# Stick-breaking logits from stacked float32r parts, and a new place for a GpSimd product, in a two-block mixer kernel

## Chip, cores and metric

The kernel runs on 1 core of one Trainium2 chip. Its metric is the device time of one execution in microseconds; "before" is the median of three runs, 1353.47 us (1352.7 to 1354.14).

## What is computed

Two blocks follow each other on a sequence of 256 tokens with 1024 channels. The first block has two layers. Each projects the normalised input `u` with one wide matrix and runs three mixers on it, A (top-k attention), B (windowed attention with sinks) and C (stick-breaking attention), gates them, merges them and adds the result to the input. The change lies in mixer C and its inputs:

```python
z = jnp.einsum('bthd,bshd->bhts', qb, k).astype(jnp.float32) * (dh ** -0.5)
log_beta = jax.nn.log_sigmoid(z)
log_1m = jnp.where(strict, jax.nn.log_sigmoid(-z), 0.0)
after = lax.cumsum(log_1m, axis=3, reverse=True) - log_1m
a = jnp.where(strict, jnp.exp(log_beta + after), 0.0)
```

There are 8 heads of 64 channels. The second block has two layers of four mixers on this stream and a context stream; its shift, scale and gate columns (`mod`) come from a matrix `w_ada_2` times a conditioning vector.

## The kernel before, in words

**Tiles.** Activations lie with channels on the partitions. A projection works on one weight tile of 256 columns: `wtile` (L226) loads it in two raw halves (`raw`, L215, on the SP queue, three buffers `wr`), ScalarE rounds each half to float32r (`wh`), VectorE takes the remainder (`wl`), four buffers each. `proj_ch` (L276) and `proj_tok` (L265) then run 48 matmuls of 256 columns, three for each product: high x high, low x high, high x low. Their PSUM pool has three buffers. Everything whose line is L107 is a matmul, whatever called it.

**Mixer C.** In `block1` (L619 to 628) two tiles give `cqT` (scaled by 1/8) and two give `ckT`, each [128, 4, 256] in float32: head 2c + a lies in chunk c on the partitions 64a to 64a + 63. Two tiles of values `cv` and two of the gate (`cg`) follow, then `stick` (L744). For each pair of chunks q and each half a it runs one pass of logits: for both key blocks s and both chunks j one float32 matmul over the 64 rows of the half, of 256 columns for s = 0 and 128 for s = 1, and after each s a bf16 mask matmul of the 256 columns on the diagonal (L759 to 762). There are 4 passes in a layer and 8 in the kernel. Between passes ScalarE, VectorE and TensorE work out logarithms, sums over later keys and exponentials.

**Mixer B** holds its parts already in float32r: `queries` (L448) cuts a tile of rotated queries into a high and a low part in the shared buffer `stg` (one buffer) and sends both with four DMAs of the SP queue to opposite halves of the two tiles `bq`; the keys, twice on the partitions, are `bk[0]` (high) and `bk[1]` (low). A logit is then two matmuls over 128 rows (`logit`, L469). `bq` lies in the places a7 and s1, `bk` in b1 and s2. A place (a tag of the pool `keep`) holds one tile at a time; a new tile in it waits until the old one was read for the last time, in the order of the program.

**GpSimd's jobs.** `ada` (L289) prepares the columns `mod` of a later layer. A job `wide` (L317) covers 512 columns: four loads `wsp` of 256 rows on the SP queue (two places, t3a and t3b), for each half k and each of nv conditioning vectors a product with a column of the vector and an addition to `acc`. With nv = 2 (the second block's) the first vector's product goes to `wc`, a tile in `stg`, and the second's overwrites `wsp` (L332 to 334). After the job `end` (L336) sums the columns of `acc` over the partitions on TensorE and VectorE writes `mod` (L342).

**What sets the order.** The tile framework puts waits between instructions in program order, and a planner fixes the order on each engine's queue at build time by an estimated timeline (`schedule_with_timeline_sim=True`, L1487). `after_tile` (L238) is called after each projection tile of `block1`. In layer 1 a counter starts at 1.0 and grows by 0.11 a call, and whenever it reaches 1 a job is taken from the list: at calls 1, 10, 19 and 28. Calls 1 to 18 are the tiles of aq/ak, av, ag, cq, ck, cv, cg, bq and bkv; mixer B stands between calls 18 and 19, calls 19 and 20 are the tiles of bg, 21 and later the merge. `end` of a job follows 10 calls later, ordered behind the last matmul at that point. In layer 0 the jobs have nv = 1 and don't use `wc`. At the end of `block1` the halves of `cT` (L1386) are loaded into t3a and t3b; the second block's context stream (`hch`, `hcl`, L525 and 526) needs `cT` and the first 16 columns of `mod`.

Of the kernel before, what the change touches and what calls it, by code (L numbers as in the profile page):

```python
# [8 lines left out]
F32 = mybir.dt.float32  # L9
F32R = mybir.dt.float32r  # L10
BF = mybir.dt.bfloat16
U8 = mybir.dt.uint8
AF = mybir.ActivationFunctionType
OP = mybir.AluOpType
# [10 lines left out]
            cq=3652, ck=4164, cv=4676, cg=5188, ma=5700, mb=6724, mc=7748)  # L25
# [33 lines left out]
class Net:  # L59
# [229 lines left out]
    def ada(self, l, blk):  # L289

        nc = self.nc
        nv = 1 if blk == 1 else 2
        wa = self.I["w_ada" if blk == 1 else "w_ada_2"][l]
        v0 = blk - 1
        mod = self.const.tile([128, 24, nv], F32, name=f"mod{blk}{l}")

        def load(n):
            return [self.raw(wa, k, n * 256, 256, True) for k in (0, 4)]

        def job(n, ws=None):  # L300
            ws = ws or load(n)
            bias = self.colB[:, 48 * (blk - 1) + 24 * l:48 * (blk - 1) + 24 * l + 24]
            p = self.P(self.pj, [128, 512])
            for k in range(8):
                g = 32 * (k % 4)
                self.mm(p[g:g + 32, :256], self.cs[:, k, :], ws[k // 4][:, k % 4, :], start=k < 4, stop=k >= 4)
            sb = self.W("adas", [128, 256], tag="score")
            nc.scalar.activation(sb, p[:, :256], AF.Copy)
            pc = self.P(self.tr, [128, 2, 4, 32])
            for j in range(2):  # L310
                self.T(pc[:, j].rearrange("p g v -> p (g v)"), sb[:, 128 * j:128 * j + 128])
            r = self.W("adar", [128, 2, nv])
            nc.vector.tensor_reduce(r, pc[:, :, :, v0:v0 + nv].rearrange("p j g v -> p j v g"), axis=AX.X, op=OP.add)
            nc.vector.scalar_tensor_tensor(mod[:, 2 * n:2 * n + 2, :], r, 0.5,
                                           bias[:, 2 * n:2 * n + 2][:, :, None].to_broadcast([128, 2, nv]),
                                           op0=OP.mult, op1=OP.add)
        def wide(n, tag):  # L317

            P = nc.gpsimd
            acc = self.K("acc", [128, 2, 512], tag=tag)  # L320
            for c in range(4):
                w = self.K("wsp", [128, 2, 512], tag=self.spare[self.nspare % len(self.spare)])
                self.nspare += 1
                nc.sync.dma_start(out=w, in_=wa[256 * c:256 * c + 256, 512 * n:512 * n + 512].rearrange(
                    "(k p) n -> p k n", p=128))
                for k in range(2):
                    for v in range(nv):
                        m = self.cs[:, 2 * c + k, v0 + v:v0 + v + 1]
                        if c == k == 0:
                            P.tensor_scalar(acc[:, v], w[:, k], m, None, op0=OP.mult)  # L330
                        else:
                            t = self.W("wc", [128, 512], tag="stg") if v + 1 < nv else w[:, k]  # L332
                            P.tensor_scalar(t, w[:, k], m, None, op0=OP.mult)  # L333
                            P.tensor_tensor(acc[:, v], acc[:, v], t, op=OP.add)  # L334

            def end():  # L336
                p = self.P(self.tr, [128, 4, 32])
                for j in range(4):
                    for v in range(nv):
                        self.mm(p[:, j, v:v + 1], acc[:, v, 128 * j:128 * j + 128], self.ones[:, 0:1])  # L340
                bias = self.colB[:, 48 * (blk - 1) + 24 * l:48 * (blk - 1) + 24 * l + 24]
                nc.vector.scalar_tensor_tensor(mod[:, 4 * n:4 * n + 4, :], p[:, :, :nv], 0.5,  # L342
                                               bias[:, 4 * n:4 * n + 4][:, :, None].to_broadcast([128, 4, nv]),
                                               op0=OP.mult, op1=OP.add)
            self.later.append((6 if nv == 1 else 10, end))

        return (mod, [lambda ws=None, n=n: job(n, ws) for n in range(12)], [lambda n=n: wide(n, ("s4", "w1")[n % 2]) for n in range(6)],
                load)

# [98 lines left out]
    def queries(self, Q, c0, src, scale):  # L448

        g = self.W("stg", [128, 2, 2, 256], F32R)  # L450
        self.tok_to_ch_split(g[:, 0], g[:, 1], src, scale)
        for a in range(2):
            r = slice(64 * a, 64 * a + 64)
            for i in range(2):
                o = 64 * (a ^ i)
                self.nc.sync.dma_start(out=Q[a][o:o + 64, c0:c0 + 2].bitcast(F32), in_=g[r, i].bitcast(F32))

    def quads(self, dst, src, scale, parts):

# [68 lines left out]
    def block1(self, l, xT, mod, pre):  # L528
        nc, V, A = self.nc, self.nc.vector, self.nc.scalar
        wi = self.I["w_in"][l]  # L530
        r = self.rstd_row(xT, EPS)
# [4 lines left out]
        u = self.pair("u", ("uh", "ul"))  # L536
# [13 lines left out]
        w = self.wtile(wi, OFF1["idx"], pre=pre.get("idx"))  # L550
# [12 lines left out]
        w = self.wtile(wi, OFF1["idx"] + 256, 68, pre=pre.get("iw"))  # L563
# [8 lines left out]
        for t in range(2):  # L572
# [3 lines left out]
            for a in range(2):  # L576
                p = self.P(self.lg, [128, 2, 256])
                b = 64 * a
# [37 lines left out]
        gate("a")  # L616
        self.finish1(ysA, gT["a"], Y["a"])

        cqT = self.K("cqT", [128, 4, 256], tag="a4")  # L619
        ckT = self.K("ckT", [128, 4, 256], tag="a5")  # L620
        for nm, dst, sc in (("cq", cqT, 0.125), ("ck", ckT, 1.0)):
            for i, w in tiles(nm, 2):
                A.activation(dst[:, 2 * i:2 * i + 2], self.proj_ch(w, u), AF.Copy, scale=sc)
        cv = self.K("cv", [128, 2, 512], tag="a6")
        for i, w in tiles("cv", 2):
            A.activation(cv[:, :, 256 * i:256 * i + 256], self.proj_tok(w, 256, u), AF.Copy)
        gate("c")
        self.stick(cqT, ckT, cv, gT["c"], Y["c"])

        bq = [self.K("bq", [128, 4, 256], F32R, tag=t) for t in ("a7", "s1")]  # L630
        bk = [self.K("bk", [128, 2, 256], F32R, tag=t) for t in ("b1", "s2")]
        bv = self.K("bv", [128, 2, 128], tag="b2")
        for i, w in tiles("bq", 2):
            ro = self.W("ro", [128, 2, 4, 64])
# [106 lines left out]
            self.nc.scalar.activation(ys[t], y, AF.Copy)  # L741
        return ys

    def stick(self, qT, kT, v, g, Y):  # L744

        nc, V, A = self.nc, self.nc.vector, self.nc.scalar
        sl = [(slice(None), slice(None), slice(128 * s, 256)) for s in range(2)]
        for q in range(2):
            es = self.K("ste", [128, 4, 2, 256], tag="at")
            for a in range(2):  # L750
                b = 64 * a
                ps = []
                x = self.K("stx", [128, 768], tag=("s3", "n2")[a])
                xs = [x[:, :512].rearrange("p (j t) -> p j t", j=2), x[:, 512:].rearrange("p (j t) -> p j t", j=2)]
                for s in range(2):
                    p = self.P(self.lg, [128, 2, 256])
                    for j in range(2):
                        c = 2 * q + j
                        self.mm(p[:, j, 128 * s:], kT[b:b + 64, c, s * 128:s * 128 + 128],  # L759
                                qT[b:b + 64, c, 128 * s:], start=j == 0, stop=False)  # L760
                    self.mm(p[:, :, 128 * s:128 * s + 128], self.identb,
                            self.bandm[:, 0:1].to_broadcast([128, 2, 128]), start=False, stop=True)
                    ps.append(p)
                    ins = A.activation(xs[s], p[sl[s]], AF.Abs)
# [727 lines left out]
```

## Time and profile before

| | |
|---|---|
| median of three runs | 1353.47 us |
| the profiled execution | 1352.58 us |
| its span, first to last instruction | 1350.8 us |
| mean granted TensorE clock | 0.972 |
| busy: TensorE matmul, VectorE, ScalarE, GpSimd | 95%, 67%, 48%, 29% |
| DMA | 217.65 MB, mean 161 GB/s |

In the profile PE is TensorE's matmuls, PEld its weight loads, DVE VectorE, ACT ScalarE, POOL GpSimd, SPq the queue that issues the DMAs. A float32 matmul leaves two matmul records, a float32r one leaves one. Matmuls overlap, so their pace is read from start to start. A releaser behind "<-" is what ended the idle time before an instruction.

### The profile page before, as it was taken

How to read it: one execution, taken by the hardware profiler on the slowest of the kernel's cores; microseconds unless marked ns; L12 is line 12 of the kernel's file. 1: busy time of each engine (PE TensorE's matmuls, PEld its weight loads, DVE VectorE, ACT ScalarE, POOL GpSimd, SP SyncE). 2: the span in 40 equal slices, each digit the busy share in tenths (PEclk: the TensorE clock that was granted, in tenths of full speed). 3: DMA queues.
4: the chain of work that ended last, by engine and by line, in shares of the span. 5: the costliest groups of instructions: out<-in, count | busy, mean ns of one | idle time of the engine just before them, and what ended most of it. 6: DMA issues, size and time to landing. Idle time of an engine off the chain costs nothing.

```text
span 1350.8 us, 27852 instructions
## 1 busy us (share of the span) xinstructions
PE 1277.5 (95%) x11386; PEld 1163.7 (86%) x11386; DVE 908.9 (67%) x1717; ACT 648.8 (48%) x1160; POOL 393.9 (29%) x233
## 2 busy tenths in 40 slices
PE   6999999999998999999998999999899999999986
PEld 2988988999898898899997988987789789999775
DVE  3897675665679855486675376754748768696873
ACT  3445456644444545764453233334736646434652
POOL 0484984150098921949500010000000000000000
PEclk8899999999989999999998999999899998999997
DMA  9764885476645575446664554326244255654220
GB/s 327 252 203 141 250 244 166 137 243 211 179 143 170 150 209 161 141 155 209 208 208 142 155 157 133 91 94 172 77 142 140 74 161 156 188 159 109 79 79 32
DMA packets 199599, 217.65 MB, mean 161 GB/s; under 512 B 10800, under 2 KB 183472, under 8 KB 198832
## 3 DMA queue, kind: packets, MB, share of 16 engines
q1 hardware_dynamic: 199472, 215.87, 53.2%
q8 instruction: 90, 1.47, 0.5%
q14 instruction: 37, 0.30, 0.1%
HBM read 199.06 MB, written 4.19 MB: 150 GB/s over the span
## 4 chain that ended last, share of the span: by engine, by line
PE 72%; DVE 12%; issue 6%; SPq 4%; DMA 3%; ACT 3%; POOL 0%; POOLq 0%; ACTq 0%; DVEq 0%
PE ps L107 68%; PE ps L111 4%; DVE wl L115 3%; SPq L466 2%; DMA wr<-w_in 2%; SPq L222 1%; DVE pe L703 1%; DVE nm L482 1%; DVE score L589 1%; ACT pe L487 1%; DMA wsp<-w_ada 1%; ACT wh L114 1%; DVE m L588 1%; DVE ro L428 1%; DVE score L584 0%
## 5 line engine op out<-in xcount | busy, mean ns | idle before, releaser
L115 DVE TENSOR_TENSOR wl<-wr,wh 128x1024 fp32r<-128x1024 f32 (+1 forms) x270 | 357.6, 1326 | 226.9 <-ACT wh L114 223.3
L114 ACT ACTIVATE wh<-wr 128x1024 fp32r<-128x1024 f32 (+1 forms) x270 | 284.9, 1056 | 349.3 <-PE ps L107 200.0
L107 PE MATMUL ps<-uh,wh 128*128 128x256 f32 x704 | 201.8, 287 | 3.4 <-ACT thm L659 3.4
L107 PE MATMUL ps<-ul,wh 128*128 128x256 f32 x704 | 201.2, 286 | 0.0
L107 PE MATMUL ps<-uh,wl 128*128 128x256 f32 x704 | 200.7, 285 | 0.0
L333 POOL TENSOR_SCALAR wsp<-wsp,cs 128x512 f32<-128x512 f32 x70 | 137.3, 1967 | 20.9 <-DMA wsp<-w_ada 20.9
L107 PEld LDWEIGHTS ps<-uh,wh 128*128 128x128 f32 x704 | 132.8, 189 | 5.8 <-ACT thm L659 4.4
L107 PEld LDWEIGHTS ps<-ul,wh 128*128 128x128 f32 x704 | 132.7, 188 | 3.1 <-issue 2.9
L107 PEld LDWEIGHTS ps<-uh,wl 128*128 128x128 f32 x704 | 132.8, 189 | 1.5 <-issue 1.1
L107 PE MATMUL ps<-wh,uh 128*128 128x256 f32 (+1 forms) x416 | 121.3, 293 | 1.8 <-ACT uh L525 1.4
L107 PE MATMUL ps<-wl,uh 128*128 128x256 f32 (+1 forms) x416 | 121.0, 292 | 1.5 <-DVE wl L115 1.5
L107 PE MATMUL ps<-wh,ul 128*128 128x256 f32 (+1 forms) x416 | 120.4, 290 | 0.4 <-DVE ul L526 0.4
L334 POOL TENSOR_TENSOR acc<-acc,wsp 128x512 f32<-128x512 f32 x70 | 107.8, 1540 | 2.5
L487 ACT ACTIVATE pe<-ps,nm 128x512 f32<-128x512 f32 (+2 forms) x160 | 85.0, 542 | 42.3 <-DVE nm L482 29.3
L397 POOL TENSOR_TENSOR rec<-rec,mhalf 128x8 f32<-128x8 f32 (+1 forms) x10 | 15.4, 1544 | 293.9 <-DVE rec L396 193.8
L482 DVE TENSOR_REDUCE nm<-ps 128x1 f32<-128x512 f32 (+2 forms) x104 | 70.8, 685 | 26.3 <-PE ps L107 24.7
L107 PEld LDWEIGHTS ps<-wh,uh 128*128 128x128 f32 x416 | 82.1, 198 | 3.7 <-ACT uh L525 1.6
L107 PEld LDWEIGHTS ps<-wl,uh 128*128 128x128 f32 x416 | 82.2, 198 | 2.8 <-DVE wl L115 1.8
L107 PEld LDWEIGHTS ps<-wh,ul 128*128 128x128 f32 x416 | 82.1, 198 | 0.8 <-DVE ul L526 0.7
L379 POOL TENSOR_TENSOR rc<-rc,mhalf 128x2 f32<-128x2 f32 x6 | 5.0, 833 | 255.4 <-DVE rc L378 255.4
L107 PE MATMUL ps<-wl,hxh 128*128 128x256 f32 x256 | 73.2, 286 | 0.5 <-DVE wl L115 0.5
L107 PE MATMUL ps<-wh,hxh 128*128 128x256 f32 x256 | 73.2, 286 | 0.1
(377 smaller groups left out, 3526.3 us busy)
## 6 DMA issues: line engine op xcount, KB each, us to landing
wr<-w_in SPq DMA_DIRECT2D x204, 512.0 KB, 4.1
wsp<-w_ada SPq DMA_DIRECT2D x68, 512.0 KB, 5.0
wr<-w_out SPq DMA_DIRECT2D x40, 512.0 KB, 3.5
wr<-w_ada SPq DMA_DIRECT2D x28, 512.0 KB, 4.5
wr<-w_br_a SPq DMA_DIRECT2D x8, 512.0 KB, 3.6
wr<-w_br_c SPq DMA_DIRECT2D x8, 512.0 KB, 4.0
wr<-w_br_b SPq DMA_DIRECT2D x8, 512.0 KB, 4.3
kC<-stg SPq DMA_DIRECT2D x64, 64.0 KB, 2.1
```

Of the source, the lines that this page charges most:

```text
L107: self.last_mm = self.nc.tensor.matmul(o, l, r, start=start, stop=stop, skip_group_check=True).ins
L111: self.nc.tensor.transpose(o, i, self.ident[:n, :n])
L114: self.nc.scalar.activation(h, x, AF.Copy)
L115: self.nc.vector.tensor_tensor(l, x, h, op=OP.subtract)
L222: self.nc.sync.dma_start(out=w[:, :, :n], in_=ap[k0 * 128:k0 * 128 + 512, c0:c0 + n].rearrange("(k p) n -> p k n", p=128))
L333: P.tensor_scalar(t, w[:, k], m, None, op0=OP.mult)
L334: P.tensor_tensor(acc[:, v], acc[:, v], t, op=OP.add)
L397: self.nc.gpsimd.tensor_tensor(r, r, self.mhalf[:, :r.shape[1]], op=OP.pow)
L428: V.tensor_tensor(dst, t1, b, op=OP.add)
L466: self.nc.sync.dma_start(out=d[32 * i:32 * i + 32].bitcast(F32), in_=g[32 * j:32 * j + 32, part].bitcast(F32))
L482: nc.vector.tensor_reduce(nmx, p, axis=AX.X, op=OP.max, negate=True)
L487: nc.scalar.activation(e[:, j, :], p[:, j, :], AF.Exp, bias=nm[:, h:h + 1], accum_out=ss[:, h:h + 1])
```

## The change

`cq` becomes two pairs of tiles, one for the high parts and one for the low parts, and `ck` one pair; each pair has a tile for each half a. `heads_ch` rounds the projection to a high part (ScalarE) and takes the low part (VectorE) in `stg`, then sends them with DMAs of SP: each part of the queries to both halves of the partitions (8 DMAs a tile), the keys' high part to the head's own half and the low part to the other half (4 a tile). A logit is two float32r matmuls over 128 rows, the stacked keys with the queries' high parts and with their low parts. The product low x low, left out in the kernel's other products, is part of it. `wc` moves from `stg` to the place w2; `bq[1]` moves from s1 to a3 and `bk[1]` from s2 to w2.

```diff
@@ wide
-                            t = self.W("wc", [128, 512], tag="stg") if v + 1 < nv else w[:, k]
+                            t = self.K("wc", [128, 512], tag="w2") if v + 1 < nv else w[:, k]
@@ new functions
+    def parts_of(self, g, l, p, scale):
+        self.nc.scalar.activation(g, p, AF.Copy, scale=scale)
+        self.nc.vector.scalar_tensor_tensor(l, p, scale, g, op0=OP.mult, op1=OP.subtract)
...
+    def heads_ch(self, dst, c0, p, scale):
+        g = self.W("stg", [128, 2, 2, 256], F32R)
+        self.parts_of(g[:, 0], g[:, 1], p, scale)
+        for a in range(2):
+            r = slice(64 * a, 64 * a + 64)
+            for i, o in ((i, o) for i in range(2) for o in range(2)):
+                if len(dst) == 2 or i == (o != a):
+                    self.nc.sync.dma_start(out=dst[i % len(dst)][a][64 * o:64 * o + 64, c0:c0 + 2].bitcast(F32),
+                                           in_=g[r, i].bitcast(F32))
+
+    def head_products(self, o, qs, k, start, swap=False):
+        for n, q in enumerate(qs):
+            self.mm(o, *((k, q) if swap else (q, k)), start=start and n == 0, stop=False)
@@ block1
-        cqT = self.K("cqT", [128, 4, 256], tag="a4")
-        ckT = self.K("ckT", [128, 4, 256], tag="a5")
-        for nm, dst, sc in (("cq", cqT, 0.125), ("ck", ckT, 1.0)):
+        stack = lambda n, tags: [self.K(n, [128, 4, 256], F32R, tag=t) for t in tags]
+        cq = (stack("cqh", ("a4", "a5")), stack("cql", ("t1", "t2")))
+        ck = (stack("ck", ("s1", "s2")),)
+        for nm, dst, sc in (("cq", cq, 0.125), ("ck", ck, 1.0)):
             for i, w in tiles(nm, 2):
-                A.activation(dst[:, 2 * i:2 * i + 2], self.proj_ch(w, u), AF.Copy, scale=sc)
+                self.heads_ch(dst, 2 * i, self.proj_ch(w, u), sc)
...
-        self.stick(cqT, ckT, cv, gT["c"], Y["c"])
-        bq = [self.K("bq", [128, 4, 256], F32R, tag=t) for t in ("a7", "s1")]
-        bk = [self.K("bk", [128, 2, 256], F32R, tag=t) for t in ("b1", "s2")]
+        self.stick(cq, ck[0], cv, gT["c"], Y["c"])
+        bq = [self.K("bq", [128, 4, 256], F32R, tag=t) for t in ("a7", "a3")]
+        bk = [self.K("bk", [128, 2, 256], F32R, tag=t) for t in ("b1", "w2")]
@@ stick
-                        self.mm(p[:, j, 128 * s:], kT[b:b + 64, c, s * 128:s * 128 + 128],
-                                qT[b:b + 64, c, 128 * s:], start=j == 0, stop=False)
+                        self.head_products(p[:, j, 128 * s:], [x[a][:, c, 128 * s:] for x in Q],
+                                           K[a][:, c, s * 128:s * 128 + 128], j == 0, True)
```

## Rows read from the trace of the kernel before

**Rows 1.** The page: engines' busy time, and the chain that ended last by engine
```profile
PE 1277.5 (95%) x11386; PEld 1163.7 (86%) x11386; DVE 908.9 (67%) x1717; ACT 648.8 (48%) x1160; POOL 393.9 (29%) x233
...
PE 72%; DVE 12%; issue 6%; SPq 4%; DMA 3%; ACT 3%; POOL 0%; POOLq 0%; ACTq 0%; DVEq 0%
```

**Rows 2.** Busy time by stage: stretch and its length, then each engine's busy us
```profile
463.00:521.00 58.00, 58.00 (x483) 55.51 (x482) 32.20 (x33) 29.73 (x40) 19.70 (x11) 1.00 0.62 182
...
535.00:586.00 51.00, 48.06 (x367) 43.12 (x366) 29.68 (x44) 33.12 (x57) 49.64 (x30) 1.00 0.52 158
604.00:659.00 55.00, 55.00 (x471) 54.70 (x471) 36.51 (x34) 21.55 (x25) 54.48 (x28) 1.00 0.62 191
```

**Rows 3.** Timeline of PE around one pass of stick-breaking logits: start, length, what
```profile
168.43 0.27 PE L107 MATMUL ps<-uh,wl 128*128 128x256 f32 x1
168.64 1.13 PE L107 MATMUL ps<-cqT,ckT 64*128 64x256 f32 x4
...
169.91 0.71 PE L107 MATMUL ps<-cqT,ckT 64*128 64x128 f32 x4
...
170.79 0.28 PE L107 MATMUL ps<-wh,ul 128*128 128x256 f32 x1
```

**Rows 4.** Mixer B's logits: PE timeline, and the list of tile bk
```profile
231.78 1.11 PE L107 MATMUL ps<-bk,bq 128*128 128x128 f32 x8
232.73 0.39 PE L107 MATMUL ps<-c_bandm,c_identb 128*128 128x512 bf16 x1
...
L107 PE MATMUL ps<-bk,bq x64: 272/278/410, 231.8 to 592.7; 128*128 128x128 f32 x32, 128*128 128x256 f32 x32
```

**Rows 5.** Tile stg: what cuts and spreads parts now (ns min/median/max), and landing
```profile
L446 DVE SCALAR_TENSOR_TENSOR stg<-ps,stg x17: 676/692/695, 184.0 to 1257.0; 128x512 fp32r<-128x512 f32 x17
L456 SPq DMA_DIRECT2D bq<-stg x16: 461/588/647, 184.4 to 533.1; - x16
...
bq<-stg SPq DMA_DIRECT2D x16, 128.0 KB, 2.6
```

**Rows 6.** Timeline of POOL, layer 1: third and fourth wide job
```profile
484.61 3.48 POOL L330 TENSOR_SCALAR acc<-wsp,cs 128x512 f32<-128x512 f32 x2 [5.31 <-PE ps L107]
535.72 1.57 POOL L333 TENSOR_SCALAR wc<-wsp,cs 128x512 f32<-128x512 f32 x1 [47.63 <-DMA bq<-stg]
...
582.85 2.59 POOL L333 TENSOR_SCALAR wsp<-wsp,cs 128x512 f32<-128x512 f32 x1
604.25 3.11 POOL L330 TENSOR_SCALAR acc<-wsp,cs 128x512 f32<-128x512 f32 x2 [18.81 <-PE ps L107]
...
657.60 1.30 POOL L334 TENSOR_TENSOR acc<-acc,wsp 128x512 f32<-128x512 f32 x1
```

**Rows 7.** Timelines of PE and DVE: job 4's column sums, mod, first context projection
```profile
678.69 1.84 PE L107 MATMUL ps<-ones,acc 128*128 128x1 f32 x16
...
683.83 0.16 DVE L342 SCALAR_TENSOR_TENSOR mod<-ps,cols 128x8 f32<-128x8 f32 x1
...
706.00 0.39 PE L107 MATMUL ps<-hch,wh 128*128 128x256 f32 x1
```

**Rows 8.** Timelines of DVE and of the SP queue where cT waits for POOL
```profile
640.67 1.22 DVE L115 TENSOR_TENSOR wl<-wr,wh 128x1024 fp32r<-128x1024 f32 x1
...
645.71 0.34 SPq L1386 DMA_DIRECT2D cT<-ctx  x1
646.14 9.28 SPq L222 DMA_DIRECT2D wr<-w_in  x4
656.20 0.37 SPq L222 DMA_DIRECT2D wr<-w_br_b  x1
658.93 0.34 SPq L1386 DMA_DIRECT2D cT<-ctx  x1
```

**Rows 9.** PE after an idle stretch, and the next stretch with its granted clock
```profile
722.62 1.08 PE L107 MATMUL ps<-wr,cs 128*32 128x256 f32 x8 [3.41 <-DMA wr<-w_ada]
...
722.70:727.90 5.20, 5.20 (x28) 4.39 (x29) 2.76 (x4) 3.18 (x5) 0.00 (x0) 0.50 0.47 141
```

More of the change, by code (lines that the diff above doesn't have):

```diff
@@ L456, in queries, with heads_tok @@
                 self.nc.sync.dma_start(out=Q[a][o:o + 64, c0:c0 + 2].bitcast(F32), in_=g[r, i].bitcast(F32))
+    def parts_of(self, g, l, p, scale):
+        self.nc.scalar.activation(g, p, AF.Copy, scale=scale)
+        self.nc.vector.scalar_tensor_tensor(l, p, scale, g, op0=OP.mult, op1=OP.subtract)
+    def heads_tok(self, dst, c0, src, scale):
+        p = self.P(self.tr, [128, 2, 2, 128])
+        for j in range(2):
+            for t in range(2):
+                self.T(p[:, j, t], src[:, t, 128 * j:128 * j + 128])
+        self.heads_ch(dst, c0, p.rearrange("p j t n -> p j (t n)"), scale)
+    def heads_ch(self, dst, c0, p, scale):
[10 more added lines that the diff above has]
+            self.mm(o, *((k, q) if swap else (q, k)), start=start and n == 0, stop=False)
     def quads(self, dst, src, scale, parts):
@@ L742, in causal_softmax, with stick @@
         return ys
-    def stick(self, qT, kT, v, g, Y):
+    def stick(self, Q, K, v, g, Y):
         nc, V, A = self.nc, self.nc.vector, self.nc.scalar
@@ L750, in stick @@
             for a in range(2):
-                b = 64 * a
                 ps = []
```

## Prediction

> **What bounds the kernel now.** I read the page first: TensorE is busy for 95% of the span and holds 72% of the chain that ended last [rows 1]. A mean hides stages, so I then read the table by stage. In the stretch where layer 1 of the first block projects the stick-breaking inputs, TensorE is busy for 58.00 of 58 us; while the stick-breaking scores are worked out, 48.06 of 51; in the merge after it 55.00 of 55 [rows 2]. VectorE is busy for about 60% there. So a matmul taken away in these stretches shortens the time, and work added to VectorE, ScalarE or the DMA queue costs nothing as long as it doesn't come late to a matmul.
>
> **The logits.** One pass (one pair of queries' chunks, one half of the partitions) stands in the timeline as four records of 256 columns, a mask matmul, four records of 128 columns and a second mask matmul. A float32 matmul leaves two records, so this is four matmuls. From the start of the last projection before it, 168.43, to the second one behind it, 170.79, are 2.36 us [rows 3]; two projection matmuls at 55.00 / 471 = 0.117 [rows 2] belong to that, so a pass with its masks takes 2.13 us. After the change a pass has eight float32r matmuls over 128 rows. The windowed mixer already runs this form: eight of them at 128 columns take 232.73 - 231.78 = 0.95 us [rows 4], 0.119 each, and 256 columns cost the 0.117 of a projection matmul. With two mask matmuls of 256 columns (taken at 0.117 each) a pass comes to 1.19 us, and 0.94 is saved. There are 2 chunks' pairs x 2 halves x 2 layers = 8 passes: 7.5 us. If a switch of form still costs 0.1 in each, 6.7. I take **7.1 us**, bounds 6.0 and 7.5. Nothing else hides these matmuls: they run on an engine that is full.
>
> **Cutting and spreading the parts.** Each of the eight projection tiles (cq and ck, two each, two layers) keeps its ScalarE copy, which now rounds, and gains one VectorE pass of 0.69 us [rows 5]: 5.5 us in all on an engine that is busy for 32.20 of 58 us there [rows 2]. Queries then need 8 DMAs a tile and keys 4, so 24 in a layer, of 128 KB. The bq tiles send the same ones: 0.59 us of queue each, landing after 2.6 [rows 5]. A query tile holds SP for 8 x 0.59 = 4.7 us. What is queued behind it on SP are the weight loads, and behind those ScalarE's and VectorE's split and the projections; POOL's loads stand in that queue too. Cover: three raw buffers and four split ones, more than one tile of 48 x 0.117 = 5.6 us of TensorE's work ahead. I cost it at nothing; without that cover each of the four query tiles could cost its 4.7 us, and I keep 0 to 3 us in all. The shared buffer stg is held by a query tile for its two cuts, the issues and the landing, some 1.4 + 4.7 + 2.6 = 8.7 us; a tile comes every 5.6 at the earliest, and the three PSUM buffers take up the 3 us of delay. The scores begin only after four more projection tiles (cv and cg), at least 22 us later, so the landing is not waited for. The gates' tiles in t1 and t2 wait for the low parts of the queries to be read, which comes before the first of them is written. These edits: 0.
>
> **GpSimd's second product.** This is the part with a hidden price. The product wc moves from stg to w2, and bk's low part moves to w2 too. The four wide jobs of layer 1 are put into the program at the 1st, 10th, 19th and 28th projection tile. The third one, at the first tile of gate b, stands behind the whole windowed mixer, so in program order its first wc comes after bk in w2 and has to wait until bk is read for the last time. Today it waits for stg: POOL begins the job at 484.61, then stands for 47.63 us until the DMA of bq has read stg, 535.72 [rows 6]. After the change it stands until the last product of bk and bq, 592.7 [rows 4], 57 us later than now. Behind it on POOL are the rest of job 3 and job 4: 535.72 to 585.44 and 604.25 to 658.90, 49.7 + 54.7 = 104.4 us of work [rows 6]. The 18.81 us that POOL waits between them falls away. So POOL ends at about 593.0 + 104.4 = 697.4 instead of 658.9. Who waits: the column sums on TensorE that now stand at 678.69, VectorE's step for mod at 683.83, and with it the second block's first context projection at 706.00 [rows 7]. The sums would come 18.7 us behind their present place.
>
> What that costs hangs on the planner. It fixes the order on each queue beforehand from its own estimate, and will put the sums behind other matmuls; the 80 us of merge and output matmuls there are enough. Then only the difference between its estimate and POOL's true pace is waited for, in order, on a full TensorE. The trace bounds that difference. In job 4 the load of cT waits on SP for POOL; it went at 645.71, 41.5 us after the job began, and the next weight load followed at once, 646.14, though its buffer had been free since 640.67 + 1.22 = 641.89 [rows 8]. The plan had POOL done before that: at least 3.8 us late, 9%. The second load of cT, 658.93, was planned behind the weight load at 656.20 [rows 8]: at most 2.7 us late in 54.7, 5%. On 104.4 us that is 5.2 to 9.4 us; I take the middle, **7 us** of waiting at the two column sums. The ends: 0, if the plan is late as well or has the sums behind all matmuls of the block; 18.7, if their place is not moved. Behind the sums now lie 22 us between mod and the first context projection [rows 7]. The context's eight chunks take three VectorE steps each, at most the 0.69 of a step of twice the size, 16.6 us in all; TensorE, itself 7 us later, takes them one by one, so I cost that at nothing (0 to 4).
>
> POOL's own pace is not fixed either: the first piece of 49.7 us ran while VectorE was busy for 29.68 of 51 us, the second of 54.7 us at 36.51 of 55 [rows 2, 6]; job 3 moves into the second kind of stretch. The Trainium skill, page "SBUF — State Buffer", section "Who interferes with whom", says that a VectorE operation with two inputs in SBUF and a GpSimd operation that reads SBUF block each other for their whole length. The two stretches agree with it, without proving it. By it job 3 would take as long as job 4.
>
> **The sum.** The profiled execution took 1352.6 us (span 1350.8 and 1.8 around it), 0.9 below the median of the runs shown. 1352.6 - 7.1 + 7.0 = 1352.5; at the median's level **1353.4 us**. A measurement of this kernel can tell some 0.2%, 2.7 us, from no change. So I forecast no change that can be told: the gain is real and is paid back in the same layer. This case's own range is 1350 to 1358.
>
> **The rivals.**
> Hidden: the plan puts the column sums late enough and POOL's lateness is covered. For it: today TensorE never waits for POOL's sums, and 38 us lie between the old and the new end of POOL in which there is other work. Against it: SP did wait for POOL [rows 8]. The time is 1353.5 - 7.1 = 1346.4; chance 0.33.
> Late chain (slower): the place is TensorE's wait for the column sum of job 4. It decides as soon as that wait passes 7.1 us. At 12% lateness, a third above the higher of the two bounds, it is 12.5 us, and a wait of that length costs clock too: after an idle of 3.41 us TensorE ran 5.2 us at a granted clock of 0.50, the 1.2 GHz level, so 2.6 us were lost [rows 9]. 1353.5 - 7.1 + 12.5 + 2.6 = 1361.5; chance 0.17.
> Blocked POOL: job 3 takes 54.7 instead of 49.7 us beside a busier VectorE, the plan doesn't know it, and 5.0 us more are waited for: 1358.4; chance 0.09. This is the mechanism that the page on SBUF names.
> No gain: the stacked form doesn't save what I think, as a pass still pays switches of form like now; 1353.5 + 7.0 - 2 = 1358.5 at worst, and 1353 if POOL is hidden as well; chance 0.04.
> My forecast keeps 0.37.
>
> **How the numbers follow.** Faster by over 0.2% (below 1350.8): all of the hidden case and a little of the forecast's own, 0.33 + 0.04 = 0.37. Slower (above 1356.2): late chain, blocked POOL, half of no gain and the upper end of the forecast's own, 0.17 + 0.09 + 0.02 + 0.06 = 0.34. The rest, 0.29, is no change. The range for 8 in 10 goes from 1345.4, the hidden case with the larger logits gain, to 1361.5, the late chain.
>
> **What would show it.** Right: in the changed profile a pass of logits lasts some 1.2 us; POOL's second product of job 3 begins right behind the last bk product, at about 585 us; POOL's last sum ends about 35 us later than 658.9; TensorE is idle for some us ahead of a column sum on an acc tile, with POOL as the releaser, and that idle about equals the logits' gain. Wrong: job 3 starts at about 490 (w2 is not shared in time), or TensorE shows no idle at these sums (hidden), or weight loads behind the new DMAs leave TensorE idle between 120 and 190 us and between 455 and 530 us (then the cover that I costed at nothing is gone).

## The result, and the profile after

The changed kernel takes 1362.25 us, the kernel before 1354.0 in runs beside it: 1.0060 of it, 95% interval 1.0045 to 1.0075. It is slower by 8 us, where I forecast no change. All intervals below are of 95%; the time varies by several us between executions of one kernel, so that a difference of two ratios is known to about 0.3%.

The page of the changed kernel, beside [rows 1]: busy times, the chain by engine and by line (its span is 1361.7 us).

```profile
PE 1276.9 (94%) x11386; PEld 1167.3 (86%) x11386; DVE 915.9 (67%) x1725; ACT 648.7 (48%) x1162; POOL 399.0 (29%) x233
...
PE 59%; DVE 13%; DMA 10%; issue 6%; ACT 5%; POOL 4%; SPq 2%; ACTq 0%; POOLq 0%; DVEq 0%
PE ps L107 56%; DMA wr<-w_in 8%; DVE wl L115 5%; PE ps L111 4%; ACT wh L114 2%; SPq L496 1%; POOL acc L334 1%; DVE pe L734 1%; DVE nm L512 1%; POOL wc L333 1%; POOL wsp L333 1%; ACT pe L517 1%; DMA wsp<-w_ada 1%; DMA xT<-x 1%; DVE score L619 1%
```

The busy time of TensorE has not fallen, and its share of the chain has, from 72% to 59%: the loads of weights (`DMA wr<-w_in`, 8%) and GpSimd (4%) took its place. Where, the waits of TensorE in block 1 show (from 60 to 725 us; columns: us in total, times, longest), first before, then after.

```profile
...
PE ps L107 <- ACT thm L659: 3.4, 2, 2.9
...
```

```profile
PE ps L107 <- ACT thm L690: 7.3, 2, 4.1
...
PE ps L107 <- POOL acc L334: 3.1, 1, 3.1
...
PE ps L107 <- DVE wl L115: 1.8, 2, 1.3
```

**The logits.** The timeline of TensorE around the pass that answers to [rows 3]:

```profile
170.53 0.28 PE L107 MATMUL ps<-uh,wl 128*128 128x256 f32 x1
170.65 0.28 PE L107 MATMUL ps<-cqh,ck 128*128 128x256 f32 x1
...
171.53 0.27 PE L107 MATMUL ps<-cql,ck 128*128 128x128 f32 x1
...
171.68 0.37 PE L107 MATMUL ps<-wh,uh 128*128 128x256 f32 x1
```

From the first product to the matmul behind the last mask it takes 1.03 us; in the kernel before it took 1.95. Read so, six of the eight passes are 0.92 shorter and two 0.81: 7.14 us in all. Read as in the prediction, from the last matmul ahead of the pass to the second one behind it, 2.36 us became 1.36: the first product now follows 0.12 us behind the matmul ahead of it and not 0.21. So read, the eight passes give 7.7 us.

**GpSimd.** POOL's timeline, beside [rows 6], and TensorE's at the column sums, beside [rows 7]:

```profile
597.05 1.57 POOL L333 TENSOR_SCALAR wc<-wsp,cs 128x512 f32<-128x512 f32 x1 [103.60 <-PE ps L107]
...
706.00 1.56 POOL L334 TENSOR_TENSOR acc<-acc,wsp 128x512 f32<-128x512 f32 x1
```

```profile
652.79 0.38 PE L107 MATMUL ps<-ones,acc 128*128 128x1 f32 x2 [3.12 <-POOL acc L334]
...
708.93 1.62 PE L107 MATMUL ps<-ones,acc 128*128 128x1 f32 x14
```

Job 3 begins behind the last product of bk, as foretold, and needs 110.5 us with job 4 instead of 104.4. TensorE stands 3.1 us for the first sum and not at all for the second.

**The weights.** Stretches of the stick-breaking inputs, layer 0 and layer 1 (as in [rows 2]; behind the five engines the granted clock, the DMA share and GB/s), before and after:

```profile
130.00:150.00 20.00, 20.00 (x174) 19.59 (x173) 11.15 (x9) 9.46 (x12) 18.50 (x10) 1.00 0.72 224
150.00:176.00 26.00, 26.00 (x216) 25.24 (x215) 15.13 (x13) 14.05 (x17) 25.00 (x15) 1.00 0.81 252
490.00:530.00 40.00, 40.00 (x313) 37.38 (x313) 21.01 (x25) 23.54 (x29) 0.00 (x0) 1.00 0.57 159
```

```profile
130.00:150.00 20.00, 20.00 (x172) 19.25 (x171) 7.37 (x9) 7.05 (x9) 12.20 (x8) 1.00 0.94 254
150.00:176.00 26.00, 25.54 (x215) 24.99 (x214) 14.83 (x14) 11.65 (x14) 17.17 (x11) 1.00 0.93 268
490.00:530.00 40.00, 40.00 (x330) 38.82 (x330) 21.79 (x25) 23.21 (x30) 3.45 (x2) 1.00 0.83 230
```

The DMA engines are nearly full for 46 us, VectorE and ScalarE run dry (11.15 to 7.37 us of 20), and the chain of the changed kernel goes from load to load (two of the pieces; columns: start, length):

```profile
151.26 7.87 DMA wr<-w_in
...
169.94 4.85 DMA wr<-w_in
```

**The wait for thm.** thm is the merge's first gate; its tanh frees the PSUM buffer that TensorE's next projection needs. ScalarE has other work ahead of it: in layer 0 of the changed kernel a table load of 1.28 us and an exponential for the last pass, a tile of weights to round, and the tanh's own table load, again 1.28 us. TensorE reaches that wait earlier by a shorter pass:

```profile
225.19 0.58 PE L107 MATMUL ps<-uh,wh 128*128 128x256 f32 x1 [3.17 <-ACT thm L690]
...
563.82 0.58 PE L107 MATMUL ps<-uh,wh 128*128 128x256 f32 x1 [4.11 <-ACT thm L690]
```

Behind it the clock falls. Stretches of the changed kernel (columns as above):

```profile
224.00:230.80 6.80, 5.62 (x26) 5.62 (x27) 1.95 (x3) 3.55 (x5) 3.95 (x3) 0.50 0.95 295
561.90:568.70 6.80, 4.88 (x23) 4.88 (x24) 2.24 (x3) 3.98 (x4) 0.00 (x0) 0.50 0.24 80
654.10:657.50 3.40, 3.40 (x19) 3.40 (x18) 0.61 (x1) 0.00 (x0) 3.40 (x4) 0.50 0.45 125
```

All three have a granted clock of 0.50, the 1.2 GHz level: one stands behind each wait for thm, one behind the wait for GpSimd. Half of TensorE's busy time in them is lost, 2.8 + 2.4 + 1.7 = 6.9 us. In the kernel before, the clock stands at 1.00 in the first two.

### The profile page after: what moved, and what is told of

It reads as the page before. It is cut to its first block, busy times and chain, and to the rows that moved or that the text cites. A ratio compares the mean times of both kernels' runs of the same rounds, so it can differ in the third digit from the quotient of the medians.

```text
span 1361.7 us, 27998 instructions
## 1 busy us (share of the span) xinstructions
PE 1276.9 (94%) x11386; PEld 1167.3 (86%) x11386; DVE 915.9 (67%) x1725; ACT 648.7 (48%) x1162; POOL 399.0 (29%) x233
## 4 chain that ended last, share of the span: by engine, by line
PE 59%; DVE 13%; DMA 10%; issue 6%; ACT 5%; POOL 4%; SPq 2%; ACTq 0%; POOLq 0%; DVEq 0%
PE ps L107 56%; DMA wr<-w_in 8%; DVE wl L115 5%; PE ps L111 4%; ACT wh L114 2%; SPq L496 1%; POOL acc L334 1%; DVE pe L734 1%; DVE nm L512 1%; POOL wc L333 1%; POOL wsp L333 1%; ACT pe L517 1%; DMA wsp<-w_ada 1%; DMA xT<-x 1%; DVE score L619 1%
## 5 line engine op out<-in xcount | busy, mean ns | idle before, releaser
L107 PE MATMUL ps<-uh,wh 128*128 128x256 f32 x704 | 204.9, 291 | 7.3 <-ACT thm L690 7.3
L107 PE MATMUL ps<-uh,wl 128*128 128x256 f32 x704 | 204.4, 290 | 0.5 <-DVE wl L115 0.5
L107 PEld LDWEIGHTS ps<-uh,wh 128*128 128x128 f32 x704 | 135.8, 193 | 8.6 <-ACT thm L690 7.7
L107 PEld LDWEIGHTS ps<-ul,wh 128*128 128x128 f32 x704 | 135.9, 193 | 3.6 <-issue 3.4
L107 PEld LDWEIGHTS ps<-uh,wl 128*128 128x128 f32 x704 | 135.8, 193 | 2.7 <-issue 1.4
L333 POOL TENSOR_SCALAR wc<-wsp,cs 128x512 f32<-128x512 f32 x28 | 53.1, 1896 | 108.0 <-PE ps L107 103.6
```

The lines of the kernel that those rows point to most:

```text
L107: self.last_mm = self.nc.tensor.matmul(o, l, r, start=start, stop=stop, skip_group_check=True).ins
```

## Experiments: the three parts apart

**Only the places.** The kernel before, with `wc` and `bk[1]` in w2 and `bq[1]` in a3.

> The kernel before with nothing but the places changed: GpSimd's second product wc and the low part of bk in w2, the low part of bq in a3. Theory (three parts: logits gain 3.5 us in each layer, the spreading DMAs cost about 7 us in a layer, GpSimd's late sums cost 4 to 8 us in layer 1): layer 0 ends as in the kernel before (its rc pow within 0.5 us of 368.12); job 3 on GpSimd starts behind the last bk product, at about 593 us; TensorE is idle for 3 to 8 us in all ahead of column sums with GpSimd as the releaser; layer 1 ends 4 to 8 us later than 710.93; the time is 1.003 to 1.006 of before. Rival 'GpSimd's lateness is covered': no idle there and a time within 0.2% of before, so that all of the loss is the spreading DMAs'.

Measured: 1.0064 (1.0040 to 1.0089). TensorE's waits:

```profile
PE ps L107 <- POOL acc L334: 3.6, 2, 2.1
```

So GpSimd's lateness is not covered. The wait is 3.6 us, at both sums, the whole loss 8.7 (5.4 to 12); the rest has no single wait in the trace. What the trace has besides are four stretches at half clock that the trace of the kernel before doesn't have, at 101.8, 426.0, 566.0 and 688.9 us, some 8 us of TensorE's time. The first of them:

```profile
101.80:108.60 6.80, 6.80 (x25) 4.86 (x25) 6.76 (x15) 3.34 (x5) 5.58 (x5) 0.50 0.29 79
```

It stands some 80 us ahead of the first tile that the edit moves, so a part of the loss may have nothing to do with the edit.

**wc in a place of its own.**

```diff
-  t = self.K("wc", [128, 512], tag="w2") if v + 1 < nv else w[:, k]
+  t = (w[:, k] if v + 1 == nv else self.W("wc", [128, 512], tag="kc") if l == 0
+       else self.K("wc", [128, 512], tag="w2"))
```

> The changed kernel, but wc lies in a place that nothing else of block 1 uses (the buffer kc of the second block). Theory of three parts: layer 0 as in the changed kernel (ends at about 372.3), GpSimd doesn't wait for bk, its sums come before they are wanted, the idle ahead of the column sums is gone, and 4 to 8 us of the changed kernel's 1362.25 come off: 1354 to 1358, 0.994 to 0.997 of the changed kernel. Rival 'the spreading DMAs carry all of it': still about 1362. Rival 'GpSimd carries all of it, in layer 0 only a shift': 1347.

Measured: 1.0019 (0.9999 to 1.0038), as the theory of three parts has it. No wait for GpSimd is left; layer 1 takes 343.0 us instead of the changed kernel's 350.6. The price of the shared place is 7.6 us by these two traces and 0.41%, 5.5 us, by the runs.

**Without the spreading DMAs.**

```diff
-  g = self.W("stg", [128, 2, 2, 256], F32R)
-  self.parts_of(g[:, 0], g[:, 1], p, scale)
...
+  for t in range(2):
+      g, l = (dst[0][t], dst[1][t]) if len(dst) == 2 else (dst[0][0], dst[0][1])
+      if t == 0 or len(dst) == 2:
+          self.parts_of(g[:, c0:c0 + 2], l[:, c0:c0 + 2], p, scale)
```

> As the kernel with wc in its own place, but the 24 spreading DMAs of a layer are left out: each part is written once over its 128 rows by ScalarE and VectorE straight into the stacked tiles, so the scores mix two heads; the eight float32r matmuls of a pass stay. Theory of three parts: the loads of the weights are as early as in the kernel before, no idle of TensorE between 130 and 190 us on a weight, layer 0 ends about 3.5 us before 368.12, layer 1 about 7 us before 710.93, and the time is about 1347, 0.995 of before. Rival 'the shorter passes themselves cost it' (the wait for thm in one piece of over 3 us behind the last pass, and 6.8 us at half clock behind it, 3.4 us lost in a layer): layer 0 still ends within 1 us of 368.12, the time is within 0.2% of before.

Measured: 1.0009 (0.9987 to 1.0032). The weights come in time again, and the time is still that of before: the rival's figure. The wait for thm is 7.3 us as in the changed kernel, with a half-clock stretch behind the second. But two more stretches at half clock stand in this trace, behind waits of 2.2 and 2.1 us for ScalarE in mixer A, where the clock is 1.00 in the kernel with `wc` alone:

```profile
100.60:110.80 10.20, 10.20 (x35) 7.42 (x35) 10.06 (x27) 4.75 (x13) 6.53 (x5) 0.50 0.50 157
438.60:448.80 10.20, 10.20 (x38) 7.74 (x36) 9.84 (x26) 4.14 (x9) 10.12 (x7) 0.50 0.41 117
```

From 60 us to the end of layer 1 TensorE idles for 4.7 us less than in that kernel, and 8 us more are lost to the clock. The execution in the profile took 1355.95 us, 4.5 above the median of its runs.

**The DMAs with the old matmuls.** The passes are `self.mm(p, K[a][b, c, ..], Q[0][a][b, c, ..])` in float32.

> As the kernel with wc in its own place, with all 24 spreading DMAs of a layer, but the scores from the high parts alone, by float32 matmuls over 64 rows, one for each product as in the kernel before (the low parts are sent and not used). Theory of three parts: weight loads late on SP and on the DMA rings, TensorE idle on them at about 150 to 180 us and again in layer 1; layer 0 ends about 7 us later than 368.12, layer 1 8 to 14 us later than 710.93, the time is 1.006 to 1.010 of before. Rival 'the shorter passes themselves cost it': without shorter passes nothing is lost, the time is within 0.2% of before.

Measured: 1.0049 (1.0031 to 1.0066), 6.6 us. That is against the rival: parts cut and spread cost without any shorter pass.

So the DMAs, which I had at nothing, cost. That a shorter pass runs into something else is so far read from traces alone.

## Experiments: the wait for thm

**VectorE empties the buffer.**

```diff
-  A.activation(thm[:, 2 * i:2 * i + 2], self.proj_ch(w, u), AF.Tanh, scale=0.5)
+  t, p = thm[:, 2 * i:2 * i + 2], self.proj_ch(w, u)
+  if mi == i == 0:
+      V.tensor_copy(t, p)
+      p = t
+  A.activation(t, p, AF.Tanh, scale=0.5)
```

> The kernel with wc in its own place, and of each layer's first merge gate tile (thm) VectorE copies the sums out of PSUM, so that TensorE gets its buffer back without waiting for ScalarE's table load and tanh, which then works in SBUF. Theory 'the shorter pass lets TensorE run into one long wait for thm, and the wait costs clock': the idle of 3.18 us at 220.9 and of 4.11 at 559.4 falls to under 1.5 us each, the half-clock stretches of 6.8 us at 223.1 and 561.0 are gone, layer 0 ends 4 to 6 us earlier than 371.3 and layer 1 8 to 12 us earlier than 714.3, the time is 1340 to 1344 where the kernel before takes 1349.3: 0.993 to 0.996. Rival 'the wait moves': TensorE is idle for as long at the next thing of ScalarE's (wh, ste), and less than 2 us are gained against the 1.0019 of the kernel with wc alone.

Measured: 0.9989 (0.9966 to 1.0011), 0.30% below the kernel with `wc` alone, where 6 to 9 per thousand were expected. The trace has the waits for ScalarE's thm down from 7.3 to 1.1 us (and 1.6 for VectorE's copy), and the clock at 1.00 in both places:

```profile
PE ps L107 <- DVE thm L693: 1.6, 2, 0.8
...
PE ps L107 <- ACT thm L695: 1.1, 1, 1.1
```

```profile
223.00:229.80 6.80, 6.59 (x48) 6.05 (x49) 4.62 (x5) 4.27 (x5) 3.47 (x3) 1.00 0.97 305
561.00:567.80 6.80, 5.41 (x35) 4.13 (x35) 3.30 (x4) 5.55 (x9) 0.00 (x0) 1.00 0.46 143
```

Why the gain is smaller than expected, the trace shows too: the clock is down in three other places, where it is at 1.00 without the copy.

```profile
102.10:108.90 6.80, 6.79 (x23) 4.94 (x24) 6.70 (x16) 2.75 (x5) 5.40 (x4) 0.50 0.32 80
597.00:600.40 3.40, 3.40 (x22) 2.84 (x22) 2.11 (x5) 1.65 (x2) 3.40 (x3) 0.50 0.00 0
678.90:682.30 3.40, 3.40 (x17) 3.24 (x16) 3.40 (x9) 0.25 (x1) 0.00 (x0) 0.50 0.75 240
```

Half of TensorE's busy time in them is 6.8 us, beside 5.0 in the two stretches that went.

> The kernel before, and VectorE copies the first merge gate tile of each layer out of PSUM in the same way. Theory: the idles for thm, 1.60 us at 221.5 and 2.94 at 559.1, go, there is no half-clock stretch behind them to save in the profile shown, so 2 to 4.5 us are gained: 0.997 to 0.9985 of before. Rival 'the wait moves to ScalarE's next tile': within 0.1% of before. If this gains as much as the same edit gains in the changed kernel, the edit says nothing of the shorter pass.

Measured: 0.9977 (0.9959 to 0.9994). The edit gains 3 us there too, and 4 in the changed kernel, which is the same within the noise. By the expectation's own last sentence this pair says nothing of the shorter pass: the edit is worth having with or without the change. Nor was the idle of 1.60 us at 221.5 one for thm: the trace puts it down to VectorE's `stx`, and to thm 0.42 us a little later.

**Nothing but shorter passes.** Without the DMAs, with `wc` apart and the copy:

> The kernel without the 24 spreading DMAs (each part written once over its 128 rows, so the scores mix two heads) and wc in its own place, and with the first thm tile of a layer copied out of PSUM by VectorE. Nothing is left but the shorter passes. Theory 'the 7.1 us of TensorE's work are real; thm's wait with the clock behind it (some 6 to 10 us) and the spreading DMAs (4.8 us of idle) eat them': no half clock at 221 and 560, 6 to 8 us less than the kernel before with the same copy (0.9977): 0.991 to 0.9935 of before. Rival 'the clock takes back what TensorE saves, wherever it saves': 0.996 to 0.999, with half-clock stretches at other places.

Measured: 0.9933 (0.9906 to 0.9959). Against the kernel before with the same copy that is 0.44%, 5.9 us (some 4 more or less), beside 7.1 by the records: the clock doesn't take the gain back. The two traces agree: between 60 us and the end of layer 1 each stands for 17 us at half clock. Against the same kernel without the copy it is 10.3 us. This is the one pair in which the copy gains clearly more than in the kernel before; a part of it may be the chance of the clock that the trace without the copy shows at 100.6 and 438.6 us.

**The wait made longer.** Before its tanh, `A.activation(thm, p, AF.Copy)` twice.

> The kernel before with the wait for thm made longer: ScalarE copies the first thm tile of a layer twice (0.60 us each) before its tanh, so TensorE's buffer comes free 1.2 us later; nothing else is changed. Theory 'a wait of over 3 us in one piece costs clock': idles of 1.60 at 221.5 and 2.94 at 559.1 grow to about 2.8 and 4.1, behind the second, maybe behind both, stands a half-clock stretch of 6.8 us which the kernel before doesn't have: 2.4 us of idle and 3.4 to 6.8 of clock, 1.004 to 1.007 of before. Rival 'only the idle counts, half-clock stretches come by chance': 2.4 us, 1.0018, within 0.1% of that.

Measured: 1.0017 (1.0000 to 1.0035). It settles nothing: in this kernel's order TensorE waits 2.97 us in layer 1, for stx and not for thm, hardly more than the 2.94 of before, so the run didn't make the wait that it was meant to. Behind that wait the clock did fall, where in the kernel before it didn't:

```profile
565.20:572.00 6.80, 6.02 (x18) 4.63 (x19) 1.06 (x3) 4.33 (x8) 6.80 (x5) 0.50 0.23 80
```

## Experiments: what of the spreading costs

**Another queue.** `nc.scalar.dma_start` instead of `nc.sync.dma_start`.

> The kernel with wc in its own place, the 24 spreading DMAs of a layer issued from ScalarE's queue and not from SP's. Theory 'SP is held, and the weight loads behind the spreading DMAs go late': TensorE's idle in layer 0 falls from 13.5 to about 11 us (that of the kernel without these DMAs), in layer 1 from 11.3 to about 9, the idle at 180 us on a stick-breaking tile and the lateness of wl of up to 6 us between 143 and 171 us are gone; 1.5 to 5 us less than the kernel with wc alone, ratio to before 0.998 to 1.001. Rival 'the DMA rings are full': idle and lateness as with SP, the ratio within 0.2% of 1.0019. Rival 'ScalarE pays': its issues hold the copies behind them, and the time is over 3 us longer.

Measured: 1.0068 (1.0046 to 1.0091). The time is that of the third theory, and the DMA share from 150 to 176 us is 0.99; that ScalarE's held copies are the cause was not followed up. The Trainium skill, page "Trainium Kernel Development and Optimization", section "Key Constraints", says that DMAs issued from several engines share the same DMA engines, so that another queue saves the issue time alone. The run agrees in so far as the other queue gained nothing; it doesn't prove the rule.

**Half the DMAs.** Each part goes straight to its own half, `self.parts_of(dst[0][a][r, c0:c0 + 2], .., p[r], scale)` for each half r, and one DMA takes it to the other.

> The kernel with wc in its own place, but ScalarE and VectorE write each part straight into its own half of the stacked tiles (two steps of 64 partitions instead of one of 128), and only the other half goes by DMA: 12 DMAs a layer instead of 24, and a query tile doesn't need the staging buffer. Theory 'the spreading DMAs cost 2 to 3 us in a layer': half of it comes back, layer 0 ends about 1.3 us before 371.3, layer 1 about 2.5 before 714.3, the DMA share between 130 and 176 us falls from 0.93 to about 0.85; ratio to before 0.999 to 1.001. Rival 'the DMAs cost nothing, the loss is in the clock and in thm': no difference to 1.0019. Rival 'the added steps on ScalarE and VectorE cost more than the DMAs': over 1.004.

Measured: 1.0042 (1.0016 to 1.0068), the figure of the second rival. TensorE stands for 4.9 us at 181 us, for the stick-breaking step `stx`; the same wait comes back below.

**Small DMAs in the same places.**

```diff
-  g = self.W("stg", [128, 2, 2, 256], F32R)
...
-  self.nc.sync.dma_start(out=dst[i % len(dst)][a][64 * o:64 * o + 64, c0:c0 + 2].bitcast(F32),
-                         in_=g[r, i].bitcast(F32))
+  self.nc.sync.dma_start(out=s[64 * o:64 * o + 64, n].bitcast(F32),
+                         in_=g[i][r, c0:c0 + 2, :8].bitcast(F32))
```

> The kernel with the shorter passes, wc in its own place and the first thm tile copied by VectorE, the parts written once over 128 rows (so the scores mix two heads); at the place of each of the 24 spreading DMAs stands one that waits for the same part and sends 8 columns of each row, a 32nd of the bytes, to a tile that nobody reads. With the DMAs whole this kernel is at 0.9989 of before, without them at 0.9933. Theory 'the bytes cost: the rings are full between 130 and 176 us (share 0.93 to 0.95) and the weights land late': 0.9925 to 0.9945, TensorE's idle from 60 us to the end of layer 0 about 2.2 us. Rival 'SP costs: the issues and their waits for ScalarE's parts hold the weight loads behind them': 0.997 to 0.9995 and an idle of about 3.7 us or more.

Measured: 0.9920 (0.9895 to 0.9946). There are as many DMAs, they hold SP as long (0.60 us each, 0.59 whole), and the cost is gone: SP's time is not what costs. Beside the whole ones (0.9989) it is 0.69% or 9.3 us, known to some 4.6. From 130 to 150 and from 150 to 176 us, whole and small:

```profile
130.00:150.00 20.00, 20.00 (x178) 19.05 (x177) 8.56 (x9) 6.00 (x9) 10.91 (x7) 1.00 0.91 250
150.00:176.00 26.00, 25.49 (x216) 25.06 (x215) 13.84 (x13) 12.18 (x14) 19.20 (x11) 1.00 0.94 270
```

```profile
130.00:150.00 20.00, 20.00 (x178) 19.09 (x177) 9.67 (x11) 7.16 (x11) 11.06 (x7) 1.00 0.54 151
150.00:176.00 26.00, 26.00 (x225) 25.95 (x224) 17.73 (x14) 14.39 (x17) 21.30 (x13) 1.00 0.95 288
```

Behind 150 us the DMA engines are as full with the small DMAs, 0.95, and TensorE is busy for all of the 26 us. So a high share did no harm by itself there. What differs is the stretch before it, with a share of 0.54 and not 0.91. From 60 us to the end of layer 1 TensorE idles for 12.7 us with the whole DMAs and for 8.8 with the small ones, so that these two traces show less than half of the 9.3.

One thing was changed along with the bytes: the small version has no staging buffer. With the whole DMAs ScalarE waits in layer 1 until they have read `stg`:

```profile
ACT stg L461 <- DMA ck<-stg: 3.7, 1, 3.7
ACT stg L461 <- DMA cql<-stg: 3.5, 1, 3.5
```

In layer 0 it is 1.2 and 0.5 us. What of the cost comes by this buffer and what by late weights was not separated.

**Half the DMAs, with the copy.**

> The kernel with wc in its own place, the first thm tile copied by VectorE, and each part written straight into its own half of the stacked tiles in two steps of 64 partitions, so that 12 DMAs a layer go instead of 24, half the bytes. Theory 'the bytes of the spreading DMAs cost': half of what lies between 0.9989 (all bytes) and 0.992 (a 32nd of them) comes back: 0.994 to 0.997. Rival 'SP waits for each of the two steps and the weights stand behind it, as in the run of this form without the copy (1.0042; TensorE idle 4.86 us at 181)': 0.999 to 1.003, and that idle is there again.

Measured: 1.0032 (1.0018 to 1.0046): the rival, and the idle is there again. It is not SP's waits for the two steps, though. The timelines of SP, POOL and PE, and the clock behind the idle:

```profile
170.14 0.42 SPq L222 DMA_DIRECT2D wr<-w_in  x1
174.16 0.37 SPq L324 DMA_DIRECT2D wsp<-w_ada  x1
174.62 9.77 SPq L222 DMA_DIRECT2D wr<-w_in  x4
...
167.73 6.40 POOL L335 TENSOR_TENSOR acc<-acc,wsp 128x512 f32<-128x512 f32 x3
...
184.64 2.08 PE L107 MATMUL ps<-stx,cf 128*128 128x512 f32 x2 [4.29 <-DVE stx L806]
```

```profile
183.50:190.30 6.80, 5.66 (x16) 4.27 (x17) 5.78 (x8) 2.59 (x4) 3.87 (x3) 0.50 0.71 211
```

SP stands from 170.56 to 174.16 for GpSimd to give back a buffer of `wsp`, with four weight loads behind it. Late weights hold ScalarE and VectorE, and with them the stick-breaking step. Whether the order on SP or GpSimd's own lateness brings this about in this form alone was not tried. So this run does not test the bytes. Its layer 1, which has no such idle, takes 339.3 us, as long as with the small DMAs (339.3) and less than with the whole ones (342.0); that goes with the theory and is one trace of each.

## Experiments: versions

> A version meant to beat both kernels: parts as in the changed kernel, but nothing is stacked and nothing is sent; high by high, low by high and high by low are three float32r products over 64 rows each (12 matmuls a pass instead of 8, so at 0.119 us a pass of 1.19 + 0.48 = 1.67 us, 0.46 less than the 2.13 of before, 3.7 us in eight passes); wc in its own place, VectorE copies the first thm tile. Theory: no idle of the spreading DMAs, no wait for GpSimd, no long wait for thm: 0.9977 - 3.7 / 1350 = 0.995, bounds 0.992 to 0.997. Rival 'float32r over 64 rows goes at half the pace': a pass of 2.6 us and 0.9985 to 1.001. Rival 'the clock takes it back': 0.997 to 0.999.

Measured: 0.9949 (0.9930 to 0.9968), the lowest of the versions that compute the whole, 6.9 us below the kernel before. But the products don't gain:

```profile
170.22 0.27 PE L107 MATMUL ps<-uh,wl 128*128 128x256 f32 x1
170.42 0.97 PE L107 MATMUL ps<-cq,ck 64*128 64x256 f32 x6
171.33 0.28 PE L107 MATMUL ps<-c_bandm,c_identb 128*128 128x256 bf16 x1
171.54 0.88 PE L107 MATMUL ps<-cq,ck 64*128 64x128 f32 x6
```

The first six one by one, in narrower stretches (the third and fourth, then the sixth):

```profile
170.76 0.40 PE L107 MATMUL ps<-cq,ck 64*128 64x256 f32 x2
...
171.12 0.28 PE L107 MATMUL ps<-cq,ck 64*128 64x256 f32 x1
```

From the third product to the sixth are 0.36 us, 0.12 each: over 64 rows they go at the pace of 128 rows, so the rival's half pace is wrong. What the theory left out are the changes between 64 and 128 rows: 0.20 us from the projection's matmul to the first product, 0.22 from the first to the second, 0.21 from the sixth to the mask and 0.21 from the mask to the next product, where products of 256 columns of one form start 0.12 apart. A pass is as long as in the kernel before, which pays the same changes.

> The kernel before with wc in the buffer kc and the first thm tile copied by VectorE, the scores as in the kernel before. In the version with three products over 64 rows a pass took as long as here (1.73 us from the first product to the last, 1.71 in the kernel before), so if its 0.9949 comes from the copy and from wc alone, this kernel comes to the same: 0.994 to 0.997. Rival 'the products over 64 rows do gain': 0.9975 to 0.9985, that of the kernel before with the copy alone (0.9977).

Measured: 0.9962 (0.9943 to 0.9981). The intervals overlap: the copy and `wc`'s place are enough to explain the version, and a gain of its products is not shown.

## Why the prediction was wrong

**The logits** were right: 7.1 us foretold, 7.1 or 7.7 in the records by where a pass is taken to begin, 5.9 in the run with nothing else.

**GpSimd's second product** was right in its mechanism and about right in its sum: 7 us foretold, 5.5 to 8.7 by the runs. The wait itself is smaller, 3.1 to 3.6 us and 1.7 of clock, and in the changed kernel it stands at job 3's sum alone; I had put 7 on both. So it is in part luck that the sum came out near. Job 3 began at 597.05 us, near the 593.0 of the working (the "about 585" in the list of signs contradicts that), and GpSimd ended at 707.6, 10 us later than foretold. GpSimd's work grew by 6.1 us, to 110.5, beside a VectorE busy for 72% of that time instead of 63%, as the rival "blocked POOL" had it. The Trainium skill's rule on that, page "SBUF — State Buffer", section "Who interferes with whom", agrees with it, without being proved: two jobs of 54.7 would be 109.4.

**The step that failed** is "Cutting and spreading the parts", costed at nothing with 0 to 3 us kept. I counted the DMAs as time on SP (4.7 us a query tile) and asked whether three raw and four split buffers cover that. SP's time is not what cost, as the small DMAs show. The bytes cost, by late weights or by the staging buffer that they hold. The DMA engines stood at 0.72 to 0.81 before, and 24 x 128 KB = 3.1 MB more in a layer filled them to 0.94. That the buffers cover a delay and not a rate, since each weight tile is loaded once, is my reading and no run tests it. The sentence on `stg` failed with it: I took the landing at 2.6 us, and the DMAs of the keys landed after 6.2 us (their median), the slowest after 9.8. By the runs the spreading costs 7.6 us (0.9989 against 0.9933), 9.3 (against 0.9920), 6.6 (with the old matmuls) and, between the two kernels with the wait for thm, 1.3. That last pair may be the clock's chance: the trace without the DMAs idles for 4.7 us less and loses 8 us more to half clock.

**What the prediction did not have** is the wait for thm. "Nothing else hides these matmuls: they run on an engine that is full" is untrue behind the last pass of a layer: there TensorE already waited for ScalarE ([rows 2] has 48.06 of 51 us busy), and in the traces the shorter pass turned into waiting, 3.4 to 7.3 us, with half clock behind it. What that costs the runs don't settle: the copy that takes the wait away gains 3.1 us in the kernel before, 4.1 with the change and its DMAs, and 10.3 without them.

By the runs, from one kernel to the next: -5.9 for the logits, +7.6 for the spreading, +1.0 for thm (4.1 less 3.1) and +5.5 for GpSimd make 8.2 us, as measured. The chain closes by its making, since each run is compared with the next; each member is known to about 4 us, and the spreading is the largest loss.

The sum of the two traces, up to the end of layer 1, where the changed kernel is 12.0 us late: -7.1 of logits, +3.9 thm, +3.1 GpSimd, +1.8 for `wl`, +6.9 of half clock, together 8.6. The 3.4 that are left have no row of their own. The time came out near the rival "late chain", 1361.5, by luck and another way: its wait is 3.1 us and not 12.5.

## What to carry to other kernels

Price a DMA twice: on its queue, and as bytes on the DMA engines in that very stretch; here, where their share was 0.72 to 0.81, bytes that arrive in time by themselves made the loads beside them late. Before a matmul is credited with its time, look at what TensorE waits for next: work removed just ahead of a wait becomes idle time, and the copy of one tile by another engine was worth 3 to 10 us here, where the matmuls were worth 6. Two uses of one place join their engines: the slow one's wait is inherited by all that stands behind the other.

## What was not expected of the hardware

The length of a wait does not settle the clock. Behind 2.94 us it stayed at 1.00 in the kernel before, behind 2.97 it fell for 6.8 us in the kernel with the longer wait, and behind 2.2 and 2.1 for 10.2 in the kernel without the DMAs. Behind 3.18 it fell in the kernel with `wc` alone, and in the kernel without the DMAs it did not:

```profile
222.00:228.80 6.80, 3.76 (x31) 3.76 (x32) 2.53 (x3) 5.83 (x7) 3.20 (x2) 1.00 0.51 155
```

So the half-clock part of a sum is a chance of some us, and one profile of each kernel doesn't measure it. And a float32r product over 64 rows goes at the pace of one over 128, 0.12 us; what costs is each change between them, some 0.2.
